# HGRN scores and scores times values: 128x128 matmuls per pair of chunks in place of 64- and 32-wide tiles

## Chip, cores and metric

One core of one Trainium2 chip runs the whole program. The metric is device time in microseconds. The kernel before takes 2924.32 us, the median of 3 runs (2922.41 to 2926.64 us). Engines are named as in the profile: PE is the matmul engine and PEld its weight loads, DVE the vector engine, ACT the scalar engine, POOL and SP the other two.

## The reference

The program is a four-part trunk over 1024 tokens of width 1024: an even layer (SSD and gMLP heads), a feed-forward layer, an odd layer (a convolution module and HGRN2 heads) and a second feed-forward layer. The change touches the HGRN2 heads of the odd layer only. There are 8 heads; in each the tokens are cut into 16 chunks of 64:

```python
qg = qv * jnp.exp(bcum - mid)
kg = k * jnp.exp(mid - bcum)
causal = jnp.tril(jnp.ones((c, c), dtype=bool))
att = jnp.where(causal, jnp.einsum("bnthk,bnshk->bnhts", qg, kg), 0.0)
o_intra = jnp.einsum("bnhts,bnshv->bnthv", att, iv)
...
def step(s, inp):
    qd, kd, vc, cd = inp
    o = jnp.einsum("blhk,bhkv->blhv", qd, s)
    s = s * cd[..., None] + jnp.einsum("blhk,blhv->bhkv", kd, vc)
    return s, o
```

So the scores of a chunk are a 64 by 64 product of `kg` and `qg` over 128 channels, kept where the key's token is not after the query's; they are multiplied with the values `iv`; the product of the queries with the running state is added. Scores between different chunks are not used.

## The kernel before

Everything is kept with channels on the 128 partitions, tokens along the free axis. Dense projections are split into a high and a low part and run as three matmuls per tile of 128 channels: `dense` (lines 149 to 151, 512 tokens at a time) and `dense_tok` (lines 160 to 162). `odd` (line 1106) runs the odd layer. For each head h it walks `hgrn_proj` (line 914), a generator over 8 units of dense work (two halves of `wf`, two halves of `wq`, four of `wig`) that yields once more at its end, and then, for h below 6, one pair of convolution channels (`conf_pair`, `conf_half`, lines 867 to 887; 4 units). Between two units `unit` (line 118) emits one step of queued small work and up to three convolution taps (`conv31`, line 889; L900, on DVE). The queued small work is `hgrn_core` (line 973) of the head before: each of its `yield`s ends a step. The tile scheduler then orders each engine's instructions by priority, mostly as they were written; weights have a higher priority.

The steps of `hgrn_core` are: transposes of `kg` (L981); the scores (L991, L993 on PE, then the masked copies L995, L998 on DVE); the state's products and its chain over the chunks in two steps (L1008 on PE, L1016 on DVE, L1017 on ACT); two empty steps; the output for two halves of 8 chunks (L1032 and L1035 on PE, L1038 on ACT, L1039 and L1040 on DVE); the norm and the store. That is 9 yields. All these matmuls have plain fp32 operands, and the trace shows two passes on PE for each.

The scores of chunk n are two matmuls: 64 keys by the chunk's last 32 queries (L991, a 128x64 tile of the array) and its first 32 keys by its first 32 queries (L993, a 128x32 tile). Even chunks land on partitions 0 to 63, odd ones on 64 to 127, so `att` of a head is 128 partitions by 8 times 64, in one buffer of [128, 512]; the two such buffers (`self.att`, lines 1110 to 1114) alternate between heads. `blk_u` is the causal mask of 64 by 64, twice (line 1256). The output step walks pairs of chunks: two matmuls of 64x64 tiles (L1032), then two of 128x64 tiles with the state (L1035), added in the same PSUM bank. PSUM has 4 banks named `mm` for dense work and 4 named `sm` for the small work.

Of the kernel before, what the change touches and what calls it, by code (L numbers as in the profile page):

```python
# [17 lines left out]
T = 1024  # L18
HALF = 512
NT = 8  # L20
# [36 lines left out]
class Trunk:  # L57
# [9 lines left out]

# [1 line left out]
    def nm(self, s):  # L69
# [27 lines left out]
    def split(self, t, h, lo):  # L97
        """t = h + lo: h holds the leading 12 bits, lo the exact remainder."""
        self.nc.scalar.copy(R(h), t)  # L99
        return self.nc.vector.tensor_tensor(R(lo), t, h, ALU.subtract)  # L100
# [17 lines left out]
    def unit(self, nsteps=1, nlow=0):  # L118
        """Called after each unit of dense work: emits queued small work."""
        for _ in range(nsteps):  # L120
            while self.steps:
                try:
                    next(self.steps[0])
                    break
                except StopIteration:
                    self.steps.popleft()
            else:
                break
        for _ in range(nlow):
            if self.lows:  # L130
                self.lows.popleft()()
# [10 lines left out]
    def dense(self, ps, w, acts, r, w0=0, ws=P, first=True, last=True):  # L142
        """ps[out channel, tokens] += W^T act over the K tiles of acts (hi, lo)."""
        wh, wl = w
        n = len(acts)
        for k, (ah, al) in enumerate(acts):
            c = slice(w0 + k * ws, w0 + k * ws + P)
            mm = self.nc.tensor.matmul
            mm(ps, R(wh[:, c]), R(ah[:, r]), start=(first and k == 0), stop=False)  # L149
            mm(ps, R(wh[:, c]), R(al[:, r]), start=False, stop=False)  # L150
            mm(ps, R(wl[:, c]), R(ah[:, r]), start=False, stop=(last and k == n - 1))  # L151

    def dense_tok(self, ps, ws, acts, t, n):
        """ps[tokens of tile t, n] = act^T W; ws are two K-half weight tiles."""
        r = slice(t * P, (t + 1) * P)
        mm = self.nc.tensor.matmul
        for k, (ah, al) in enumerate(acts):
            wh, wl = ws[k // 4]
            c = slice((k % 4) * n, (k % 4) * n + n)
            mm(ps[:, :n], R(ah[:, r]), R(wh[:, c]), start=(k == 0), stop=False)  # L160
            mm(ps[:, :n], R(ah[:, r]), R(wl[:, c]), start=False, stop=False)  # L161
            mm(ps[:, :n], R(al[:, r]), R(wh[:, c]), start=False, stop=(k == len(acts) - 1))  # L162

    def lnexp(self, after):
        """Loads the activation table set that serves both Ln and Exp, after the given instruction."""
        with self.tc.issue_after(after.ins):
            self.nc.scalar.preload_act_table_set("natural_log_exp_and_others")

    def rstd(self, src, out, scale, shape):
        """out = (src * scale + eps) ** -0.5, with one Newton step."""  # L170
        nc = self.nc
        vv = self.small(shape, "rs_v%d" % shape[1])
        tt = self.small(shape, "rs_t%d" % shape[1])
        nc.vector.tensor_scalar(vv, src, scale, EPS, ALU.mult, ALU.add)
        nc.scalar.activation(tt, vv, AF.Ln)
        nc.scalar.activation(out, tt, AF.Exp, scale=-0.5)
        nc.scalar.activation(tt, out, AF.Square)
        nc.vector.tensor_tensor(tt, tt, vv, ALU.mult)
        nc.vector.tensor_scalar(tt, tt, -0.5, 1.5, ALU.mult, ALU.add)
        nc.vector.tensor_tensor(out, out, tt, ALU.mult)  # L180

    def psum_parts(self, acc, r):
        """Sum over the partitions, given to every partition."""
        n = r.stop - r.start
# [3 lines left out]

# [1 line left out]
    def norm_start(self, X, g, split=True):  # L190
# [32 lines left out]
    def scaled_split(self, x, g, h, lo):  # L223
        """x * g = h + lo."""
        self.nc.scalar.activation(R(h), x, AF.Copy, scale=g)  # L225
        self.nc.vector.scalar_tensor_tensor(R(lo), x, g, h, ALU.mult, ALU.subtract)

    def norm_rows(self, st, square=False):
        """The norm's factor of every token, on every partition (or its square); takes the place of the sums."""
        for half in range(2):  # L230
# [6 lines left out]

# [1 line left out]
    def wino_start(self, X, g, spill):  # L239
        return dict(X=X, g=g, acc=None, spill=spill, ops={}, late=[])  # L240

    def wino_ops(self, st, r, k):
        """Operands of channel tiles k and k + 4; X is overwritten (the residual is in st["spill"])."""
        nc, X, tt = self.nc, st["X"], self.nc.vector.tensor_tensor
# [32 lines left out]

# [1 line left out]
    def out_chunk(self, wsrc, acts, X, norm=None, fill=0, segs=(hs(0), hs(1))):  # L279
        """X += W^T acts for chunks of four K tiles (wsrc, acts: one per chunk), in blocks of two output tiles.  # L280
        norm: state of the norm that follows; then segment after segment of the tokens."""
        nc = self.nc
# [33 lines left out]

# [1 line left out]
    def ffn_in(self, l, st, hid, load):  # L318
        """hid = relu(W1^T h)^2 in Winograd's form over 2 x 2 quadrants (output tiles, K halves, token halves)."""
        nc, ops, tt = self.nc, st["ops"], self.nc.vector.tensor_tensor  # L320
# [13 lines left out]
        def weights():  # L334
            """The seven operands of one unit after the other, in the order of their use."""
            def op(src):
# [120 lines left out]

# [1 line left out]
    def dt_prep(self, after):  # L459
# [53 lines left out]
    def gmlp(self, st):  # L513
# [37 lines left out]
        def first(r):  # L551
            """Operands of one segment of tokens, without the norm's factor."""
            for i in range(NT):
# [6 lines left out]
        def factors():  # L560
            """The norm's factor, tokens on the partitions."""
            ps = self.sm_ps()
# [278 lines left out]

# [1 line left out]
    def lower_bound(self):  # L843
# [70 lines left out]
    def hgrn_proj(self, h, acts):  # L914
        """Projections of head h and the elementwise work on its gates; a generator over dense units."""
        nc, a = self.nc, self.a
# [56 lines left out]
    def hgrn_core(self, h, hd):  # L973
# [9 lines left out]
        yield  # L983
        at = self.att[h % 2]
        at3 = at.rearrange("p (c t) -> p c t", t=64)
        ps = self.sm_ps()
        ps3 = ps.rearrange("p (c t) -> p c t", t=64)
        for n in range(16):
            j, p = n % 2, n // 2
            m0 = n * 64  # L990
            nc.tensor.matmul(ps[64 * j:64 * j + 64, p * 64 + 32:p * 64 + 64], kg[:, m0:m0 + 64],  # L991
                             qg[:, m0 + 32:m0 + 64], start=True, stop=True)
            nc.tensor.matmul(ps[64 * j:64 * j + 32, p * 64:p * 64 + 32], kg[:, m0:m0 + 32],  # L993
                             qg[:, m0:m0 + 32], start=True, stop=True)
        nc.vector.copy_predicated(at3[:, :, 32:64], bcast_mid(self.blk_u[:, 32:64], NT), ps3[:, :, 32:64])  # L995
        for j in range(2):
            pr = slice(64 * j, 64 * j + 32)
            nc.vector.copy_predicated(at3[pr, :, 0:32], bcast_mid(self.blk_u[pr, 0:32], NT), ps3[pr, :, 0:32])  # L998
        yield
        V = [self.slot("V"), self.slot("V")]  # L1000
# [24 lines left out]
        for half in range(2):  # L1025
            r = hs(half)
            ps = self.sm_ps()
            for c in range(4):
                p = half * 4 + c
                for j in range(2):  # L1030
                    pr = slice(64 * j, 64 * j + 64)
                    nc.tensor.matmul(ps[pr, b(c)], at[pr, p * 64:p * 64 + 64], iv[pr, b(p)], start=True, stop=False)  # L1032
                for j in range(2):
                    n = 2 * p + j
                    nc.tensor.matmul(ps[64 * j:64 * j + 64, b(c)], qg[:, n * 64:(n + 1) * 64], vv(n),  # L1035
                                     start=False, stop=True)
            s2 = self.small([P, HALF], "s2")
# [11 lines left out]
    def hgrn_load(self, h, gate):  # L1049
        """Head h's output, channels on the partitions, split."""  # L1050
        nc = self.nc
# [126 lines left out]

# [1 line left out]
    def build(self):  # L1180
# [37 lines left out]

# [1 line left out]
def layout(inputs):  # L1220
# [34 lines left out]
    blk = np.zeros((P, P), np.float32)  # L1255
    blk[:64, :64] = blk[64:, :64] = tri[:64, :64]
    r["cmat"] = np.concatenate([eye, tri, np.ones((P, P), np.float32), blk], axis=1)
# [38 lines left out]
```

## Time and profile before

| what | value |
|---|---|
| median of 3 runs | 2924.32 us |
| span of the profiled execution, first to last instruction | 2924.2 us |
| PE busy | 2892.0 us, 99% of the span |
| PEld busy | 2398.8 us, 82% |
| DVE busy | 1923.9 us, 66% |
| ACT busy | 1194.7 us, 41% |
| mean granted clock of PE | 0.985 |

The span is the only time known of the profiled execution; it lies 0.1 us from the median of the runs, so times read from the trace can be set against the runs directly. Busy times of PE are of little use by themselves, since matmuls overlap: a dense matmul lasts 0.39 us in the trace and the next starts 0.23 us after it. What a block of matmuls costs is read from the start of its first to the start of the matmul that follows it. The granted clock is 1.00 at the higher of PE's two levels (2.4 GHz) and 0.50 at the lower (1.2 GHz).

### The profile page before, as it was taken

How to read it: one execution, taken by the hardware profiler on the slowest of the kernel's cores; microseconds unless marked ns; L12 is line 12 of the kernel's file. 1: busy time of each engine (PE TensorE's matmuls, PEld its weight loads, DVE VectorE, ACT ScalarE, POOL GpSimd, SP SyncE). 2: the span in 40 equal slices, each digit the busy share in tenths (PEclk: the TensorE clock that was granted, in tenths of full speed). 3: DMA queues.
4: the chain of work that ended last, by engine and by line, in shares of the span. 5: the costliest groups of instructions: out<-in, count | busy, mean ns of one | idle time of the engine just before them, and what ended most of it. 6: DMA issues, size and time to landing. Idle time of an engine off the chain costs nothing.

```text
span 2924.2 us, 37621 instructions
## 1 busy us (share of the span) xinstructions
PE 2892.0 (99%) x15149; PEld 2398.8 (82%) x15149; DVE 1923.9 (66%) x2961; ACT 1194.7 (41%) x1964; POOL 4.0 (0%) x16
## 2 busy tenths in 40 slices
PE   8999998999999999999999999999999999999998
PEld 8988786788888888889888888888778788888887
DVE  5666878669444576537787888774587644566546
ACT  6422424237655422215343333444356655522112
POOL 0000000000000000000000000000000000000000
PEclk9999999999999999999999999998999999999999
DMA  4131425413333632212111111112512333453211
GB/s 159 45 120 62 130 87 176 134 58 108 115 116 115 209 132 100 101 51 87 61 50 50 53 57 51 50 38 66 194 51 101 116 115 116 137 202 115 87 58 59
DMA packets 100031, 287.30 MB, mean 98 GB/s; under 512 B 10768, under 2 KB 33680, under 8 KB 99856
## 3 DMA queue, kind: packets, MB, share of 16 engines
q1 hardware_dynamic: 83440, 242.47, 25.1%
q10 hardware_dynamic: 16416, 42.42, 3.7%
q8 instruction: 119, 1.95, 0.3%
q14 instruction: 56, 0.46, 0.0%
HBM read 217.61 MB, written 67.24 MB: 97 GB/s over the span
## 4 chain that ended last, share of the span: by engine, by line
PE 97%; DVE 1%; ACT 1%; DMA 0%; issue 0%; SPq 0%; DVEq 0%
PE mm L149 20%; PE mm L150 20%; PE mm L151 20%; PE mm L330 6%; PE mm L331 6%; PE mm L332 6%; PE mm L160 3%; PE mm L161 3%; PE mm L162 3%; PE sm L991 1%; PE sm L331 1%; PE sm L330 1%; PE sm L332 1%; PE sm L993 1%; PE sm L1035 1%; PE sm L1032 1%
## 5 line engine op out<-in xcount | busy, mean ns | idle before, releaser
L293 DVE TENSOR_TENSOR x<-x,mm 128x512 f32<-128x512 f32 (+1 forms) x416 | 258.7, 624 | 301.2 <-PE mm L151 292.4
L99 ACT CAST wh<-wr 128x1024 fp32r<-128x1024 f32 (+1 forms) x180 | 188.7, 1049 | 617.4 <-PE mm L150 554.0
L149 PE MATMUL mm<-fh,wh 128*128 128x512 f32 (+1 forms) x1152 | 424.9, 369 | 0.0
L151 PE MATMUL mm<-fh,wl 128*128 128x512 f32 (+1 forms) x1152 | 423.6, 368 | 0.0
L150 PE MATMUL mm<-fl,wh 128*128 128x512 f32 (+1 forms) x1152 | 422.4, 367 | 0.0
L149 PE MATMUL mm<-hh,wh 128*128 128x512 f32 x960 | 390.5, 407 | 0.0
L151 PE MATMUL mm<-hh,wl 128*128 128x512 f32 x960 | 383.4, 399 | 0.0
L150 PE MATMUL mm<-hl,wh 128*128 128x512 f32 x960 | 383.2, 399 | 0.0
L900 DVE SCALAR_TENSOR_TENSOR cy<-ag,vec,cy 128x1023 f32<-128x1023 f32 (+14 forms) x240 | 303.9, 1266 | 4.0
L100 DVE TENSOR_TENSOR wl<-wr,wh 128x1024 fp32r<-128x1024 f32 (+1 forms) x180 | 220.0, 1223 | 76.4 <-ACT wh L99 76.0
L151 PEld LDWEIGHTS mm<-fh,wl 128*128 128x128 f32 x1152 | 216.7, 188 | 38.5
L150 PEld LDWEIGHTS mm<-fl,wh 128*128 128x128 f32 x1152 | 216.5, 188 | 38.2
L149 PEld LDWEIGHTS mm<-fh,wh 128*128 128x128 f32 x1152 | 216.9, 188 | 36.9
L160 PE MATMUL mm<-wh,hh 128*128 128x256 f32 (+1 forms) x768 | 219.1, 286 | 8.6 <-ACT hh L225 8.6
L149 PEld LDWEIGHTS mm<-hh,wh 128*128 128x128 f32 x960 | 184.6, 192 | 44.7 <-issue 3.7
L150 PEld LDWEIGHTS mm<-hl,wh 128*128 128x128 f32 x960 | 184.2, 192 | 41.9 <-issue 1.8
L151 PEld LDWEIGHTS mm<-hh,wl 128*128 128x128 f32 x960 | 183.7, 191 | 42.5
L161 PE MATMUL mm<-wl,hh 128*128 128x256 f32 (+1 forms) x768 | 217.2, 283 | 0.4 <-DVE wl L100 0.4
L162 PE MATMUL mm<-wh,hl 128*128 128x256 f32 (+1 forms) x768 | 216.2, 283 | 0.0
L330 PE MATMUL mm<-T,wq 128*128 128x512 f32 x512 | 201.1, 394 | 0.6 <-ACT snap L379 0.6
L331 PE MATMUL mm<-T,wq 128*128 128x512 f32 x512 | 201.2, 394 | 0.0
L332 PE MATMUL mm<-T,wq 128*128 128x512 f32 x512 | 200.3, 393 | 0.0
(301 smaller groups left out, 5157.5 us busy)
## 6 DMA issues: line engine op xcount, KB each, us to landing
wr<-in_w_dram SPq DMA_DIRECT2D x134, 512.0 KB, 3.6
hid<-hid ACTq DMA_DIRECT2D x64, 512.0 KB, 3.5
ft<-hid SPq DMA_DIRECT2D x64, 512.0 KB, 4.7
x<-xd SPq DMA_DIRECT2D x24, 512.0 KB, 10.2
A<-acs_d SPq DMA_DIRECT2D x16, 512.0 KB, 5.9
wr<-in_wig_dram SPq DMA_DIRECT2D x16, 512.0 KB, 3.6
wr<-in_wxbc_dram SPq DMA_DIRECT2D x12, 512.0 KB, 3.5
wr<-in_wv_dram SPq DMA_DIRECT2D x8, 520.0 KB, 5.2
```

The source lines that it names most:

```text
L100: return self.nc.vector.tensor_tensor(R(lo), t, h, ALU.subtract)
L149: mm(ps, R(wh[:, c]), R(ah[:, r]), start=(first and k == 0), stop=False)
L150: mm(ps, R(wh[:, c]), R(al[:, r]), start=False, stop=False)
L151: mm(ps, R(wl[:, c]), R(ah[:, r]), start=False, stop=(last and k == n - 1))
L160: mm(ps[:, :n], R(ah[:, r]), R(wh[:, c]), start=(k == 0), stop=False)
L161: mm(ps[:, :n], R(ah[:, r]), R(wl[:, c]), start=False, stop=False)
L162: mm(ps[:, :n], R(al[:, r]), R(wh[:, c]), start=False, stop=(k == len(acts) - 1))
L293: nc.vector.tensor_tensor(X[o][:, r], X[o][:, r], ps, ALU.add)
L330: mm(ps, R(w[:, c]), R(b[:, L]), start=(first and k == 0), stop=False, skip_group_check=not first)
L331: mm(ps, R(w[:, c]), R(b[:, H]), start=False, stop=False, skip_group_check=not first)
L332: mm(ps, R(w[:, cl]), R(b[:, L]), start=False, stop=(last and k == 3), skip_group_check=not first)
L900: nc.vector.scalar_tensor_tensor(d, st[:, :T - k], w, d, ALU.mult, ALU.add)
```

## The change

The scores become one matmul per pair of chunks: 128 keys by 128 queries (both chunks), 4 of them per PSUM bank, so two banks and two steps per head. The off-diagonal 64x64 blocks are computed and not copied. `att` of a head is now two buffers of [128, 512], one for each half, each holding 4 blocks of 128x128 with zeros outside the masks; both heads in turn use the same two buffers. The mask `blk` becomes block-diagonal. The masked copies are three per half instead of three per head. Scores times values is one 128x128 matmul per pair, 4 in a row, followed by the 8 matmuls with the state in a row. `hgrn_core` has 10 yields instead of 9. Other differences in the diff are comments.

```diff
@@ hgrn_core
-        at = self.att[h % 2]
-        at3 = at.rearrange("p (c t) -> p c t", t=64)
-        ps = self.sm_ps()
-        ps3 = ps.rearrange("p (c t) -> p c t", t=64)
-        for n in range(16):
-            j, p = n % 2, n // 2
-            m0 = n * 64
-            nc.tensor.matmul(ps[64 * j:64 * j + 64, p * 64 + 32:p * 64 + 64], kg[:, m0:m0 + 64],
-                             qg[:, m0 + 32:m0 + 64], start=True, stop=True)
-            nc.tensor.matmul(ps[64 * j:64 * j + 32, p * 64:p * 64 + 32], kg[:, m0:m0 + 32],
-                             qg[:, m0:m0 + 32], start=True, stop=True)
-        nc.vector.copy_predicated(at3[:, :, 32:64], bcast_mid(self.blk_u[:, 32:64], NT), ps3[:, :, 32:64])
-        for j in range(2):
-            pr = slice(64 * j, 64 * j + 32)
-            nc.vector.copy_predicated(at3[pr, :, 0:32], bcast_mid(self.blk_u[pr, 0:32], NT), ps3[pr, :, 0:32])
-        yield
+        at = self.att
+        for half in range(2):
+            ps = self.sm_ps()
+            for c in range(4):
+                m = b(half * 4 + c)
+                nc.tensor.matmul(ps[:, b(c)], kg[:, m], qg[:, m], start=True, stop=True)
+            v4 = lambda t: t.rearrange("p (c j t) -> p c j t", j=2, t=64)
+            m4 = bcast_mid(self.blk_u, 4).rearrange("p c (j t) -> p c j t", j=2)
+            nc.vector.copy_predicated(v4(at[half])[:, :, :, 32:64], m4[:, :, :, 32:64], v4(ps)[:, :, :, 32:64])
+            for j in range(2):
+                pr = slice(64 * j, 64 * j + 32)
+                nc.vector.copy_predicated(v4(at[half])[pr, :, j, 0:32], m4[pr, :, j, 0:32], v4(ps)[pr, :, j, 0:32])
+            yield
...
-                for j in range(2):
-                    pr = slice(64 * j, 64 * j + 64)
-                    nc.tensor.matmul(ps[pr, b(c)], at[pr, p * 64:p * 64 + 64], iv[pr, b(p)], start=True, stop=False)
-                for j in range(2):
-                    n = 2 * p + j
-                    nc.tensor.matmul(ps[64 * j:64 * j + 64, b(c)], qg[:, n * 64:(n + 1) * 64], vv(n),
-                                     start=False, stop=True)
+                nc.tensor.matmul(ps[:, b(c)], at[half][:, b(c)], iv[:, b(p)], start=(c == 0), stop=False, skip_group_check=True)
+            for n in range(half * 8, half * 8 + 8):
+                pr = slice(64 * (n % 2), 64 * (n % 2) + 64)
+                nc.tensor.matmul(ps[pr, b((n // 2) % 4)], qg[:, n * 64:(n + 1) * 64], vv(n), start=False, stop=True,
+                                 skip_group_check=True)
@@ layout
-    blk[:64, :64] = blk[64:, :64] = tri[:64, :64]
+    blk[:64, :64] = blk[64:, 64:] = tri[:64, :64]
```

On PE, at the score step of head 0, the order before is the end of a dense unit and then the two small matmuls of each chunk in turn (`hh`, `hl` are the activations, `wh`, `wl` the weights; the last numbers are output partitions and columns):

```order
L149 MATMUL mm_11734<-hh_5766,wh_11682 128x512
L150 MATMUL mm_11734<-hl_5758,wh_11682 128x512
L151 MATMUL mm_11734<-hh_5766,wl_11683 128x512
L991 MATMUL sm_11762<-qg_11307,kg_11308 64x32
L993 MATMUL sm_11762<-qg_11307,kg_11308 32x32
```

The same place in the changed kernel:

```order
L151 MATMUL mm_11734<-hh_5766,wl_11683 128x512
L989 MATMUL sm_11762<-qg_11307,kg_11308 128x128 x4
L149 MATMUL mm_11797<-hh_5759,wh_11792 128x512
L150 MATMUL mm_11797<-hl_5751,wh_11792 128x512
L151 MATMUL mm_11797<-hh_5759,wl_11793 128x512
```

The 32 small matmuls have become 4, and dense work follows at once; 24 dense matmuls later the other 4 stand in the same way.

On PE, at the output step of head 0, before (the second half follows after 48 more matmuls of L160 to L162):

```order
L162 MATMUL mm_12078<-wh_11964,hl_5758 128x256
L1032 MATMUL sm_12132<-iv_11325,att_10866 64x128 x2
L1035 MATMUL sm_12132<-V_11851,qg_11307 64x128 x2
L1032 MATMUL sm_12132<-iv_11325,att_10866 64x128 x2
L1035 MATMUL sm_12132<-V_11851,qg_11307 64x128 x2
```

and in the changed kernel:

```order
L162 MATMUL mm_12112<-wh_11914,hl_5758 128x256
L1027 MATMUL sm_12166<-iv_11325,att_10866 128x128 x4
L1030 MATMUL sm_12166<-V_11860,qg_11307 64x128 x8
L1027 MATMUL sm_12186<-iv_11325,att_10868 128x128 x4
L1030 MATMUL sm_12186<-V_11861,qg_11307 64x128 x8
L149 MATMUL mm_12221<-hh_5759,wh_12210 128x512
```

The first half has moved behind the last dense unit of the projections (one more yield stands ahead of it), so the two halves now follow each other; and the kinds of matmul change once per half, not once per pair.

On DVE, from the score step of head 0 in the changed kernel (`cy` are convolution taps, `hA` and `hB` the gates of the next head):

```order
L992 COPY_PREDICATED att_10866<-cm,sm_11762 128x8x32
L995 COPY_PREDICATED att_10866<-cm,sm_11762 32x4x32 x2
L900 SCALAR_TENSOR_TENSOR cy_11619<-ag_10896,vec,cy_11619 128x1010
L900 SCALAR_TENSOR_TENSOR cy_11619<-ag_10896,vec,cy_11619 128x1009
L900 SCALAR_TENSOR_TENSOR cy_11619<-ag_10896,vec,cy_11619 128x1008
L933 TENSOR_TENSOR hA_11686<-hA_11686,hB_11687 128x1024
L992 COPY_PREDICATED att_10868<-cm,sm_11823 128x8x32
L995 COPY_PREDICATED att_10868<-cm,sm_11823 32x4x32 x2
```

Before, one set of three copies stood there, with the taps and `hA` after it; now a second set waits for the second score block.

## Rows read from the trace of the kernel before

**Rows 1.** The page, part 1 and part 4: busy time, and the chain by engine.
```profile
PE 2892.0 (99%) x15149; PEld 2398.8 (82%) x15149; DVE 1923.9 (66%) x2961; ACT 1194.7 (41%) x1964; POOL 4.0 (0%) x16
...
PE 97%; DVE 1%; ACT 1%; DMA 0%; issue 0%; SPq 0%; DVEq 0%
```
**Rows 2.** Windows, score step to score step, heads 0 to 5: busy, clock, DMA.
```profile
1481.27:1567.56 86.29, 86.29 (x551) 71.84 (x551) 76.75 (x87) 34.45 (x59) 0.20 (x1) 0.96 0.15 49
...
sum 497.34, PE 497.34 PEld 414.27 DVE 405.77 ACT 202.98 POOL 1.23; mean PE 82.89 PEld 69.05 DVE 67.63 ACT 33.83 POOL 0.20
```
**Rows 3.** Timeline of PE, score step of head 0: start, us, operation.
```profile
1480.72 0.40 PE L150 MATMUL mm<-hl,wh 128*128 128x512 f32 x1
1480.95 0.39 PE L151 MATMUL mm<-hh,wl 128*128 128x512 f32 x1
1481.27 0.30 PE L991 MATMUL sm<-qg,kg 128*64 128x32 f32 x2
...
1481.68 0.30 PE L991 MATMUL sm<-qg,kg 128*64 128x32 f32 x2
...
1488.46 0.80 PE L149 MATMUL mm<-hh,wh 128*128 128x512 f32 x1
...
1489.49 0.63 PE L151 MATMUL mm<-hh,wl 128*128 128x512 f32 x1
1489.91 0.63 PE L149 MATMUL mm<-hh,wh 128*128 128x512 f32 x1
```
**Rows 4.** Windows, the eight score steps: first, and sum.
```profile
1481.27:1488.46 7.19, 7.19 (x65) 5.72 (x64) 2.22 (x2) 5.79 (x7) 0.00 (x0) 0.86 0.23 74
...
sum 61.83, PE 61.83 PEld 49.01 DVE 14.17 ACT 42.81 POOL 0.00; mean PE 7.73 PEld 6.13 DVE 1.77 ACT 5.35 POOL 0.00
```
**Rows 5.** Windows, end of score step to end of low clock, eight heads.
```profile
1488.46:1493.25 4.79, 4.79 (x13) 3.81 (x12) 4.53 (x6) 0.00 (x0) 0.00 (x0) 0.50 0.00 0
...
sum 35.08, PE 35.08 PEld 27.95 DVE 30.35 ACT 2.61 POOL 0.00; mean PE 4.38 PEld 3.49 DVE 3.79 ACT 0.33 POOL 0.00
```
**Rows 6.** Timeline of PE, output step of head 0, first half.
```profile
1521.49 0.44 PE L1032 MATMUL sm<-iv,att 64*64 64x128 f32 x4
1521.86 0.44 PE L1035 MATMUL sm<-V,qg 128*64 128x128 f32 x4
...
1524.43 0.39 PE L160 MATMUL mm<-wh,hh 128*128 128x256 f32 x1
```
**Rows 7.** Timeline of PE, blocks of the even layer: gMLP mix, SSD diagonal.
```profile
207.51 5.52 PE L611 MATMUL sm<-wst,v 128*128 128x128 f32 x48
212.79 0.48 PE L149 MATMUL mm<-hh,wh 128*128 128x512 f32 x1
...
395.06 1.09 PE L724 MATMUL sm<-A,xd 128*64 128x128 f32 x16
396.09 0.50 PE L149 MATMUL mm<-hh,wh 128*128 128x512 f32 x1
```
**Rows 8.** Instructions of L611: ns min, median and max.
```profile
L611 PEld LDWEIGHTS sm<-wst,v x128: 186/192/193, 166.4 to 212.6; 128*128 128x128 f32 x128
L611 PE MATMUL sm<-wst,v x128: 271/275/377, 166.4 to 212.8; 128*128 128x128 f32 x128
```
**Rows 9.** Windows, transposes and outputs of head 7 without dense work; L611 block.
```profile
2057.98:2064.83 6.85, 6.85 (x73) 3.94 (x72) 2.69 (x4) 1.86 (x3) 0.00 (x0) 1.00 1.03 410
207.51:212.79 5.28, 5.28 (x50) 5.28 (x48) 4.89 (x8) 1.58 (x2) 0.00 (x0) 1.00 0.35 99
```
**Rows 10.** Instructions of L995 and L998, the masked copies: ns, counts.
```profile
L995 DVE COPY_PREDICATED att<-cm,sm x8: 440/441/444, 1488.6 to 2041.5; 128x256 f32<-128x256 uint32 x8
...
L998 DVE COPY_PREDICATED att<-cm,sm x16: 420/428/446, 1489.0 to 2042.3; 32x256 f32<-32x256 uint32 x16
```
**Rows 11.** Waits: us in total, times, longest.
```profile
DVE att L995 <- PE sm L993: 45.7, 8, 6.3
```
**Rows 12.** Windows, head 7's score step to the end of its outputs.
```profile
2034.17:2072.00 37.83, 36.14 (x248) 27.35 (x248) 20.77 (x45) 15.91 (x34) 0.00 (x0) 0.91 0.74 284
```

## The prediction

> **What bounds the kernel now.** I read the page first. PE is busy for 99% of the span and the chain that ended last runs over PE for 97% of it [rows 1]; the other engines wait for PE far more than it waits for them. So the question is what PE spends on the work that is changed, and whether another engine is close behind.
>
> For the second half of that I read the windows from one score step to the next. Heads 0 to 5, where convolution taps run beside the projections, take 497.34 us; PE fills all of it and DVE 405.77 us, 82%. Head 0 alone has 76.75 us of DVE work in 86.29 us [rows 2]. DVE has room, but not much. Part of its idle time is the wait of the masked copy for the last score matmul, 45.7 us over 8 heads, 5.7 us each [rows 11].
>
> Then the timeline of PE at the score step of head 0. Dense matmuls start 0.23 us apart; from the last of them to the first score matmul it is 0.32 us, so changing to the small tile costs 0.09 us. One chunk (L991 and L993, two passes each) takes 1481.27 to 1481.68, 0.41 us, although it streams only 32 columns per pass; 16 chunks should be done in 6.6 us. The next dense matmul starts at 1488.46, after 7.19 us, and dense matmuls are then 0.42 us apart, nearly double [rows 3]. The granted clock explains both: its mean over the step is 0.86, and after the step it is 0.50 until 1493.25 [rows 4, 5]. So the clock falls to 1.2 GHz while the array is fed with these small matmuls alone. It happens in all eight heads: the eight steps take 61.83 us [rows 4], and the stretches behind them, mostly dense work at half clock, 35.08 us [rows 5].
>
> Last, the output step. Half a head takes 1521.49 to 1524.43, 2.94 us, and its kinds of matmul change every 0.37 us [rows 6].
>
> **The change part by part.** All of it lies on PE's path in the odd layer, so what a block takes from its start to the next matmul's start counts in full.
>
> *Scores.* Removed: 61.83 us, and 8 changes to the small tile, 0.7 us. Added: 16 blocks of 4 matmuls, 8 passes each, fp32, 128x128, 128 columns. The gMLP mix has just this form: 48 passes in 212.79 - 207.51 = 5.28 us, 0.110 us a pass, at clock 1.00 [rows 7, 9]. A block is then 0.88 us and 16 are 14.1 us. Saved: 61.83 + 0.7 - 14.1 = 48.4 us.
>
> This price carries most of the forecast, so here is what speaks against it. L611's weight load lasts 0.19 us and its matmul 0.27 us [rows 8], yet they come every 0.110 us: load and multiplication of neighbours overlap. The Trainium skill's page "TensorEngine Tiling (Array Packing)" says, under Key Properties, that different tiles can execute loads and matmuls in parallel, and its Overview promises up to twofold speed for a contraction or free size of 64 or less. By that rule the small tiles are the fast form, and a full tile gives the overlap up: rival 3 below, 2936 us. By the rows a full tile overlaps as well: 2845 us. The trace does not agree with the rule here, so I take the rows.
>
> *Clock.* If the score step is two blocks of 0.88 us with 24 dense matmuls between, nothing like the thin matmuls that preceded the fall is left (in head 0 a mean of 0.86 over 7.19 us makes 2.0 us at half clock, so some 5.2 us of them came first). What shows that the new blocks keep the clock up: the 5.28 us of L611 without dense work ran at 1.00, and so did 6.85 us of transposes and outputs of head 7 [rows 9]. The 35.08 us at half clock go by at full clock: 35.08 x (1 - 0.23/0.42) = 15.9 us saved.
>
> *Output step.* Removed: 16 x 2.94 = 47.0 us. Added per half: 8 full passes, 0.88 us, one change of kind, 0.09 us, and 16 passes of 128x64 tiles in a row. SSD's diagonal has that form: 395.06 to 396.09, 1.03 us, its own change back included [rows 7]. That is 2.00 us, 32.0 us for 16. Saved: 15.0 us. Nearly as much would come from the grouping alone, since 16 small passes in a row cost 1.03 us where four times 0.37 us were paid.
>
> *Masked copies.* Three per head, 0.44 + 2 x 0.43 = 1.3 us [rows 10], become six; two of each three are half as wide. They cost between half of today's and the same, so 0.5 to 1.3 us more DVE work per head. No PE work waits for them soon: in head 0 the scores ended at 1488.46 and were read from 1521.49 on, 33 us later [rows 3, 6]. They are free as long as DVE keeps up.
>
> *The extra step.* The second score block pushes the rest of the core back by one unit. In the heads before the last, the first output half moves behind the last dense unit; the state's chain gets as many units as before, and 4 us of outputs follow each other, which rows 9 cover. For head 7, PE had 1.7 us of idle time in 37.83 us [rows 12]; now its two output halves move among the dense matmuls of the out projection. I bound this by -1.7 us (that idle time goes) and +6 us (eight links of the state chain stand bare) and take 0, because dense work now stands between chain and output.
>
> *Buffers.* `att` is no longer doubled over heads. The next head's copy must wait for this head's outputs, behind which PE has five dense units of 24 matmuls before the next score step comes: nothing. The score banks are two per head, not one, of four; each is read by DVE within a unit: nothing.
>
> Sum: 48.4 + 15.9 + 15.0 = 79.3 us. From the span of 2924.2 us, which is the runs' median to 0.1 us, that leaves **2844.9 us**.
>
> **Rivals.**
>
> *1. DVE becomes the bound.* PE would need 497.34 - 79.3 x 6/8 = 437.9 us for heads 0 to 5; DVE has 405.77 us and about 5 us of new copies, 94% of that. Head 0 would have 76.4 us of PE and 77.6 us of DVE. If the idle time that is not the wait for scores (9.5 - 5.7 = 3.8 us) also stays, such a head takes 81.4 us, 5 us more. Two heavy heads lose 10 us: 2855 us. Against it: over six heads DVE has room, PE filled every one of these windows so far [rows 2], and the wait for scores vanishes.
>
> *2. The clock still falls.* Two outputs in a row, or a score block near other small work, could be thin enough. Then the 15.9 us stay: 2861 us. Against it: rows 9.
>
> *3. A full tile does not overlap (slower).* If the new passes paid load and multiplication one after the other, 0.19 + 0.275 = 0.467 us, the 256 full passes (128 for scores, 128 for values) would cost 119.6 us instead of 28.2 us: 2936 us, 12 us slower than before. It decides from 0.42 us a pass on. For it: they read operands that ACT and DVE have just written, with four per bank. Against it: L611 at 0.110 us.
>
> *4. More gain.* If a full pass cost no more than a 128x64 one in a row (1.03/16 = 0.064 us), 256 passes would save another 11.7 us: 2833 us.
>
> **How the numbers follow.** Forecast 0.74, DVE 0.13, clock 0.08, slower 0.03, more gain 0.02. The likeliest gives 2845 us. The range reaches down to 2835 us (the tail's bound and most of rival 4) and up to 2859 us (DVE, and the tail's +6 us); the clock rival and the slow one stay out, with a little of the rest, under 2 in 10. A measurement of this kernel can tell about 0.2%, 6 us, from no change. Only rival 3 is slower: 0.03; cases 1, 2 and 4 are far below 2918 us, so faster has 0.96; 0.01 is left for same.
>
> **What would show it.** Right: each score block lasts 0.8 to 0.9 us from its start to the next dense matmul; the granted clock shows no fall between 1400 and 2100 us and its mean rises above 0.99; half a head's outputs take about 2.0 us; a head takes about 76 us. Wrong: PE waits for DVE or ACT in heads 0 to 2, dense matmuls 0.42 us apart behind the outputs, or full passes well over 0.110 us.

## The result and the profile after

The changed kernel takes **2852.68 us** (median of 4 runs, 2851.08 to 2856.86), the kernel before 2925.31 us beside it (2922.41 to 2926.64): a ratio of 0.9757, 95% interval [0.9743, 0.9771]. In a second job (the repeat, below) it took 2852.83 us (2848.45 to 2853.66), ratio 0.9749 [0.9734, 0.9763], with the same two new waits of PE, 7.7 and 1.5 us. The forecast was 2845 us, the range 2835 to 2859 us.

The profiled execution is the slowest of the first four runs, 2856.86 us with a span of 2855.1 us. So the time of a run is 1.8 us more than its span, and the span of 2924.2 us that the forecast started from belongs to a run a little above its median; as the time of a run the forecast would be some 1.8 us higher. Below, spans are set against spans.

The page of the changed kernel, part 1 and part 4, against [rows 1]:

```profile
PE 2815.4 (99%) x14637; PEld 2361.8 (83%) x14637; DVE 1927.6 (68%) x2985; ACT 1198.3 (42%) x1964; POOL 4.0 (0%) x16
...
PE 93%; DVE 5%; ACT 1%; DMA 1%; issue 1%; SPq 0%; DVEq 0%
```

PE has 76.6 us less to do and is still busy for 99% of the span. The chain that ended last now runs for 7% over DVE, ACT and a DMA, where it was 2%.

Windows of the changed kernel, first score block to first score block, heads 0 and 3 and the sum over heads 0 to 5, against [rows 2]. The columns are the length, the busy time of PE, PEld, DVE, ACT and POOL with counts, the granted clock, the DMA share and GB/s:

```profile
1482.96:1559.43 76.47, 76.47 (x488) 66.87 (x487) 75.57 (x89) 34.55 (x59) 0.20 (x1) 1.00 0.17 56
...
1712.57:1792.75 80.18, 78.67 (x488) 68.18 (x487) 67.57 (x82) 34.73 (x59) 0.20 (x1) 0.98 0.17 53
...
sum 446.09, PE 444.58 PEld 389.08 DVE 409.83 ACT 210.38 POOL 1.23; mean PE 74.10 PEld 64.85 DVE 68.30 ACT 35.06 POOL 0.21
```

Head 0 went from 86.29 to 76.47 us and runs at clock 1.00 from end to end. PE fills it, although DVE is busy for 75.57 us of it. Head 3 is 3.7 us longer than its neighbours, at a clock of 0.98; PE has 1.5 us of idle time there.

Timeline of PE in the changed kernel, the first score block of head 0, against [rows 3]:

```profile
1482.73 0.39 PE L151 MATMUL mm<-hh,wl 128*128 128x512 f32 x1
1482.96 1.05 PE L989 MATMUL sm<-qg,kg 128*128 128x128 f32 x8
1483.77 0.48 PE L149 MATMUL mm<-hh,wh 128*128 128x512 f32 x1
```

The block takes 1482.96 to 1483.77, 0.81 us, for 8 passes: 0.10 us each. It starts 0.23 us after the dense matmul before it, the usual distance: there is no gap for a change of tile. Fifteen of the 16 blocks take 0.80 or 0.81 us, one 0.98 us.

Timeline of PE in the changed kernel, the output step of head 0, both halves, against [rows 6]:

```profile
1521.06 1.05 PE L1027 MATMUL sm<-iv,att 128*128 128x128 f32 x8
1522.04 1.09 PE L1030 MATMUL sm<-V,qg 128*64 128x128 f32 x16
1523.06 1.16 PE L1027 MATMUL sm<-iv,att 128*128 128x128 f32 x8
1524.15 1.09 PE L1030 MATMUL sm<-V,qg 128*64 128x128 f32 x16
1525.17 0.50 PE L149 MATMUL mm<-hh,wh 128*128 128x512 f32 x1
```

A head's outputs take 4.11 us in place of 5.88. The eight falls of the clock behind the score steps [rows 5] are gone.

Two things are there that were not there before. PE's waits in the changed kernel (total, times, longest):

```profile
PE sm L1055 <- DMA ol<-hgd: 7.6, 1, 7.6
...
PE sm L1030 <- ACT V L1014: 1.5, 2, 1.0
```

The first stands at the end of the heads. Timeline of PE there (in brackets the idle time before an operation, and what ended it):

```profile
1962.53 1.09 PE L1030 MATMUL sm<-V,qg 128*64 128x128 f32 x16
1971.25 1.94 PE L1055 MATMUL sm<-cm,ol 128*128 128x128 f32 x8 [7.63 <-DMA ol<-hgd]
1972.98 1.91 PE L1027 MATMUL sm<-iv,att 128*128 128x128 f32 x8
1974.83 1.83 PE L1030 MATMUL sm<-V,qg 128*64 128x128 f32 x16
1976.59 0.50 PE L149 MATMUL mm<-hyh,wh 128*128 128x512 f32 x1
```

L1055 transposes a head's output that was stored to DRAM and is loaded again for the out projection (`hgrn_load`, L1050). PE's order has these transposes between the two output halves of head 6, so the second half waits with them, and all dense work behind it. Where the load was is on SP's queue. Its timeline in the changed kernel (start, time to the end of the last of the group):

```profile
1925.94 38.35 SPq L107 DMA_DIRECT2D wr<-in_woh_dram  x4
1964.38 1.33 SPq L1050 DMA_DIRECT2D ol<-hgd  x3
```

Four loads of the out projection's weights stand ahead of the first `ol`. The later ones wait until a buffer `wr` is free; the first load of `ol` is issued at 1964.38, and PE goes on 6.9 us later.

The second is in head 3. Timeline of DVE in the changed kernel, the end of the state's chain there:

```profile
1751.98 1.25 DVE L900 SCALAR_TENSOR_TENSOR cy<-ag,vec,cy 128x1001 f32<-128x1001 f32 x1
1753.15 1.22 DVE L100 TENSOR_TENSOR wl<-wr,wh 128x1024 fp32r<-128x1024 f32 x1
1754.29 0.34 DVE L1013 SCALAR_TENSOR_TENSOR Z<-Z,hcf,sm 128x128 f32<-128x128 f32 x1
1754.55 1.22 DVE L100 TENSOR_TENSOR wl<-wr,wh 128x1024 fp32r<-128x1024 f32 x1
1755.68 0.34 DVE L1013 SCALAR_TENSOR_TENSOR Z<-Z,hcf,sm 128x128 f32<-128x128 f32 x1
```

and of PE at the same time:

```profile
1753.69 0.88 PE L1030 MATMUL sm<-V,qg 128*64 128x128 f32 x12
1755.12 0.43 PE L1030 MATMUL sm<-V,qg 128*64 128x128 f32 x2 [0.55 <-ACT V L1014]
1756.51 0.43 PE L1030 MATMUL sm<-V,qg 128*64 128x128 f32 x2 [0.96 <-ACT V L1014]
1756.87 0.50 PE L149 MATMUL mm<-hh,wh 128*128 128x512 f32 x1
```

The last links of the chain (L1013) come one at a time between convolution taps and weight splits, DVE without a gap. PE needs the last two states before they are there: its last state products take 1753.69 to 1756.87, 3.2 us in place of 1.0.

Behind both waits the clock is low. Windows of the changed kernel, dense work behind head 3's outputs, and from the load's arrival to the next dense matmul:

```profile
1756.87:1761.30 4.43, 4.43 (x14) 3.47 (x13) 4.43 (x7) 2.29 (x4) 0.20 (x1) 0.62 0.43 162
1971.25:1976.59 5.34, 5.34 (x33) 4.93 (x33) 1.50 (x2) 1.37 (x2) 0.00 (x0) 0.52 0.14 55
```

The work of the second window takes 2.95 us at full clock in the run e11_pool_load below (1964.07 to 1967.02), so the low clock costs 2.4 us more.

### The profile page after: what moved, and what is told of

The parts are those of the page before. It is cut to its first block, busy times and chain, and to the rows that moved or that the text cites. A ratio compares the mean times of both kernels' runs of the same rounds, so it can differ in the third digit from the quotient of the medians.

```text
span 2855.1 us, 36628 instructions
## 1 busy us (share of the span) xinstructions
PE 2815.4 (99%) x14637; PEld 2361.8 (83%) x14637; DVE 1927.6 (68%) x2985; ACT 1198.3 (42%) x1964; POOL 4.0 (0%) x16
## 4 chain that ended last, share of the span: by engine, by line
PE 93%; DVE 5%; ACT 1%; DMA 1%; issue 1%; SPq 0%; DVEq 0%
PE mm L149 19%; PE mm L151 19%; PE mm L150 19%; PE mm L330 6%; PE mm L331 6%; PE mm L332 6%; PE mm L160 3%; PE mm L161 3%; PE mm L162 3%; DVE cy L900 2%; PE sm L331 1%; PE sm L330 1%; PE sm L332 1%; PE sm L724 1%; PE sm L186 1%
## 5 line engine op out<-in xcount | busy, mean ns | idle before, releaser
L149 PE MATMUL mm<-hh,wh 128*128 128x512 f32 x960 | 384.5, 400 | 0.0
L100 DVE TENSOR_TENSOR wl<-wr,wh 128x1024 fp32r<-128x1024 f32 (+1 forms) x180 | 219.9, 1223 | 75.4 <-ACT wh L99 75.1
L160 PE MATMUL mm<-wh,hh 128*128 128x256 f32 (+1 forms) x768 | 219.7, 287 | 9.6 <-ACT hh L225 8.7
L162 PE MATMUL mm<-wh,hl 128*128 128x256 f32 (+1 forms) x768 | 216.7, 283 | 0.0
```

## Experiments

The theory after the result: PE's stream sets the time, and the terms for scores, clock and outputs are right; what is missing is lost in two new waits that the tenth step brings (the runs bear this out for the first wait only). The rivals: DVE has become the bound of the heavy heads; the new passes cost more than their blocks show; the gain of the outputs is one of the full tile, not of the grouping. The kernel before took 2923.79 us in the first job (7 runs) and 2924.95 us in the second.

**e1_nine_steps**: the changed kernel with one empty step less, so nine as before.

```diff
@@ hgrn_core
-        yield
         yield
         o = self.slot("o")
```

> The changed kernel with one of the two empty steps of hgrn_core left out, so that the core has nine steps again, as before the change. Theory (the tenth step pushed head 7's schedule: on SP two more weight loads stand ahead of the first load of a stored head, so PE waits 7.6 us for it and runs 10 us at half clock): the wait of the transposes for the load of hgd and the fall of the clock near 1966 us are gone, some 10 us, 2843 us. Rival (the load is late whatever the order, or the outputs, one unit earlier, now wait for the state's chain): 2853 us or more.

Measured: **2843.44 us** (2841.47 to 2846.86), ratio 0.9726 [0.9711, 0.974]. It beats both kernels: 9.2 us less than the changed one. Its SP queue:

```profile
1920.13 14.37 SPq L107 DMA_DIRECT2D wr<-in_woh_dram  x2
1934.60 0.38 SPq L1049 DMA_DIRECT2D ol<-hgd  x1
```

Two weight loads, not four, stand ahead of the first `ol`; it is issued 30 us earlier, and PE no longer waits for it: its transposes start at 1959.89. The second `ol` is issued at 1960.67, behind two more weight loads, and PE waits 1.7 us for that one. Timeline of PE, and the window from there on:

```profile
1967.37 1.06 PE L1054 MATMUL sm<-cm,ol 128*128 128x128 f32 x8 [1.69 <-DMA ol<-hgd]
```

```profile
1967.37:1973.55 6.18, 6.18 (x45) 5.34 (x45) 4.47 (x12) 3.40 (x8) 0.00 (x0) 1.00 0.96 351
```

No low clock follows this wait. Head 3's wait is gone as well, and the clock does not fall between 1400 and 2100 us. Heads 0 to 4 take 76.4 to 76.7 us. So leaving the tenth step out is worth 9.2 us here. This run takes both waits away together; the next two take one each.

**e11_pool_load**: ten steps, only the load of `ol` goes through another queue (and the small memset that stood on that queue moves to DVE).

```diff
-        nc.gpsimd.memset(vv(0), 0.0)
+        nc.vector.memset(vv(0), 0.0)
...
-            nc.sync.dma_start(o, self.hgd[h])
+            nc.gpsimd.dma_start(o, self.hgd[h])
```

> The changed kernel with its ten steps; only the queue of the last stage's loads is another: ol is loaded by GpSimd's queue instead of SP's, and the memset of V's first block is done by VectorE instead of GpSimd, so that nothing stands ahead of the loads on GpSimd. Theory (the first ol load is late because two woh loads stand ahead of it on SP and wait for a wr buffer): the load starts soon after its head was stored, at about 1923 us instead of 1964 us, PE's 7.6 us wait for it is gone, and so is the fall of the clock at 1966 us (2.5 us); 2852.7 - 10 = about 2843 us. Rival (the wait is only moved: PE comes to the second half of head 6's outputs before VectorE or ScalarE are done, whatever the load does): another wait of several us stands at the same place and the time stays at 2850 us or above.

Measured: 2844.94 us (2844.33 to 2847.36), ratio 0.9726 [0.9712, 0.9741]. Timeline of POOL and then of PE:

```profile
1926.67 0.66 POOL L1050 DMA_DIRECT2D ol<-hgd  x1 [944.17 <-ACT kt L982]
```

```profile
1963.05 1.09 PE L1030 MATMUL sm<-V,qg 128*64 128x128 f32 x16
1964.07 1.09 PE L1055 MATMUL sm<-cm,ol 128*128 128x128 f32 x8
...
1967.02 0.50 PE L149 MATMUL mm<-hyh,wh 128*128 128x512 f32 x1
```

The load is issued at 1926.67, PE does not wait, and the clock does not fall there. Expected were 10 us, measured 7.8 us; heads 4 and 5 are 1.5 us longer together (77.18 and 60.62 us, against 76.46 and 59.84), and PE waits for V there too, 0.3 us each. Head 3 keeps its wait (80.47 us, 0.3 us more). That SP's order is the cause of the long wait is shown; the rival's other wait at that place did not appear.

**e8_half_taps**: ten steps, and less work for DVE beside the heads: 15 of the 31 taps are left out.

```diff
-        for k in range(31):
+        for k in range(16):
```

> The changed kernel with its ten steps, and 16 of the 31 taps of the convolution that VectorE works through beside the heads; the other 15 taps of every channel are left out. Theory (head 3's wait for the multiply of V is VectorE being late, as taps stand between the links of the chain; in heads 0 to 2 TensorE still sets the length): PE's waits for ScalarE at V in the heads are gone with the half clock behind them, no head of the first five is longer than 76.7 us, none shorter than 76.2 us, and the 7 us wait for the load of ol stays, if the order on SP is the same; about 2849 us. Rival (VectorE sets the length of heads 0 to 2 as well): heads 0 to 2 shrink clearly below 76 us.

Measured: 2845.96 us in one run. Windows of heads 0 and 3:

```profile
1477.68:1554.15 76.47, 76.47 (x487) 66.87 (x486) 48.10 (x64) 34.38 (x59) 0.20 (x1) 1.00 0.17 56
...
1707.29:1783.74 76.45, 76.45 (x487) 66.90 (x486) 48.12 (x64) 34.36 (x59) 0.21 (x1) 1.00 0.18 56
```

With DVE at 48 us a head, head 0 takes 76.47 us as before, to the hundredth, and head 3 has come down from 80.18 to 76.45 us. So a DVE that is busy for 75.6 of 76.5 us costs nothing in head 0, and one that is busy for 67.6 us costs 3.7 us in head 3: what stands between the chain's links decides, not the busy share. The load's wait stays, 6.6 us. The single time is 3 us below what was expected. Some 2.3 us of that is not of the taps' doing: the first score block starts at 1477.68, against 1479.95 in the repeat, and from 455 to 500 us, in the even layer, the mean clock is 0.96 against 0.89. The rest lies behind the heads, where the wait is 1 us shorter and the low clock at it lasts 6.8 us in place of 10.2.

**e10_scores_twice**: nine steps, each score matmul issued twice.

```diff
-                nc.tensor.matmul(ps[:, b(c)], kg[:, m], qg[:, m], start=True, stop=True)
+                for _ in range(2):
+                    nc.tensor.matmul(ps[:, b(c)], kg[:, m], qg[:, m], start=True, stop=True)
```

> The changed kernel with nine steps, in which every score matmul is issued twice into the same place (same output). It doubles the 0.81 us of a score block, 16 blocks. Theory (TensorE's stream alone sets the time in the heads, so an added matmul pass is paid in full): 16 x 0.81 = 13 us more than the 2843.4 us of the nine-step kernel, 2856.5 us, and a head is 1.6 us longer (78.1 us instead of 76.5). Rival (VectorE, busy 75.5 of 76.5 us in the first heads, sets a head's length there): the added passes are taken up in heads 0 to 2, some 5 us of them, and the time is 2851 us or less.

Measured: 2856.0 us (2854.06 to 2856.58), ratio 0.976 [0.9744, 0.9777]; 12.6 us more than e1_nine_steps. Timeline of PE and the window of head 0:

```profile
1480.08 1.95 PE L990 MATMUL sm<-qg,kg 128*128 128x128 f32 x16
1481.78 0.48 PE L149 MATMUL mm<-hh,wh 128*128 128x512 f32 x1
```

```profile
1480.08:1558.33 78.25, 78.25 (x503) 68.66 (x502) 77.52 (x90) 34.80 (x59) 0.21 (x1) 1.00 0.17 55
```

The doubled block takes 1.70 us, 0.89 us more, and head 0 is 1.78 us longer, two such blocks. An added pass is paid in full in the heavy heads too. DVE is not their bound.

**e3_scores_only**: the new scores with the old output step, pair by pair on small tiles.

```diff
-                nc.tensor.matmul(ps[:, b(c)], at[half][:, b(c)], iv[:, b(p)], start=(c == 0), stop=False, skip_group_check=True)
-            for n in range(half * 8, half * 8 + 8):
...
+                for j in range(2):
+                    pr = slice(64 * j, 64 * j + 64)
+                    nc.tensor.matmul(ps[pr, b(c)], at[half][pr, c * P + 64 * j:c * P + 64 * j + 64], iv[pr, b(p)], start=True, stop=False)
+                for j in range(2):
+                    n = 2 * p + j
+                    nc.tensor.matmul(ps[64 * j:64 * j + 64, b(c)], qg[:, n * 64:(n + 1) * 64], vv(n),
+                                     start=False, stop=True)
```

> The changed kernel with the old output step (64x64 and 128x64 tiles in turn, pair by pair) on the new scores. Theory (the output step is worth 15 us by itself, 2.94 against 2.0 us per half, and the scores with the clock the rest): 2853 + 15 = 2868 us. Rival (5.9 us of alternating small matmuls in a row now let the clock fall in each head, 3 to 10 us of half clock): 2880 us or more. Rival (PE waits for something else behind the output step, so its price is hidden): 2853 us.

Measured: 2865.95 us (2862.06 to 2866.45), ratio 0.9797 [0.9781, 0.9814]. Windows of head 0's outputs and of the whole of head 3:

```profile
1519.15:1525.03 5.88, 5.88 (x66) 3.14 (x65) 5.25 (x9) 3.42 (x8) 0.18 (x1) 1.00 0.54 178
1716.14:1794.43 78.29, 78.29 (x504) 66.45 (x502) 66.37 (x81) 34.57 (x59) 0.20 (x1) 1.00 0.17 54
```

The scores alone bring 57.8 us, the outputs the other 13.3 us (2865.95 - 2852.68); by the blocks the outputs are 8 x (5.88 - 4.11) = 14.2 us. That the two agree is in part chance: here head 3 does not wait, though this kernel has ten steps (78.29 us, and head 0 78.34), while the load's wait is here as well (6.3 us, with 13.7 us of low clock). Head 0 against head 0, the outputs are worth 78.34 - 76.47 = 1.87 us, 15.0 us for eight heads. The outputs on small tiles, 5.88 us in a row, leave the clock at 1.00, as the new ones do.

**e4_grouped_small**: the changed kernel with the values' product on 64x64 tiles, but eight matmuls in a row.

```diff
-                nc.tensor.matmul(ps[:, b(c)], at[half][:, b(c)], iv[:, b(p)], start=(c == 0), stop=False, skip_group_check=True)
+                for j in range(2):
+                    pr = slice(64 * j, 64 * j + 64)
+                    nc.tensor.matmul(ps[pr, b(c)], at[half][pr, c * P + 64 * j:c * P + 64 * j + 64], iv[pr, b(p)],
+                                     start=(c == 0), stop=False, skip_group_check=True)
```

> The changed kernel with scores times values as eight 64x64 matmuls in a row per half in place of four 128x128. Theory (the gain of the output step comes from grouping, not from the full tile): a block of 16 passes in a row costs as SSD's diagonal, about 1.0 us, against 0.93: 2854 us. Rival (the full tile is what helps): 0.18 us per pass as before the change, 1.5 us a block, 2862 us or more. Rival (small tiles packed in a row are faster than a full tile): 0.55 us a block, 2847 us.

Measured: 2851.93 us (2848.76 to 2854.93), ratio 0.9753 [0.9739, 0.9768], the same as the changed kernel. Timeline of PE, first half of head 0's outputs:

```profile
1521.07 0.28 PE L162 MATMUL mm<-wh,hl 128*128 128x256 f32 x1
1521.28 1.09 PE L1029 MATMUL sm<-iv,att 64*64 64x128 f32 x16
1522.30 1.09 PE L1033 MATMUL sm<-V,qg 128*64 128x128 f32 x16
```

Sixteen small passes take 1.02 us, the eight full ones of the changed kernel 0.98 or 1.09 us; the small ones also need 0.09 us more after the dense matmul (1521.07 to 1521.28, where the usual distance is 0.12). So the outputs gain by the grouping, and the full tile adds little: head 3 takes 77.25 us here, 2.9 us less than in the changed kernel, and without that the small form would be some 2 us slower (an estimate: 2.9 less the 0.75 us between the medians). The Trainium skill, page "TensorEngine Tiling (Array Packing)", section Overview, promises up to twofold speed for a dimension of 64 or less; this run agrees for one pass (0.064 us against 0.12), but the 64-wide tiles need twice the passes here. It holds for passes of one kind in a row: pair by pair, four such passes cost 0.37 us [rows 6], 0.09 us each.

**e5_thin_split**: the kernel before, its thin scores cut into two steps of eight chunks, one empty step less.

```diff
@@ hgrn_core (before)
+            if n == 7:
+                yield
...
-        yield
```

> The kernel before, its thin score matmuls unchanged, but in two steps of eight chunks with a dense unit between (one empty step left out, so nine steps). It tells the clock's share from that of the form. Theory (the fall of the clock comes from 5 us of thin matmuls in a row): each half takes 3.3 us at full clock and no fall follows: 8 x (7.73 - 6.75) + 16 = 24 us less, 2901 us. Rival (the clock falls all the same, behind one of the halves): 2925 us, or slower with two falls per head.

Measured: 2909.87 us (2905.13 to 2913.21), ratio 0.9951 [0.9936, 0.9965]. Windows of head 0's first half, its second half, and what follows:

```profile
1481.05:1484.33 3.28, 3.28 (x34) 2.62 (x33) 3.28 (x3) 3.26 (x5) 0.00 (x0) 1.00 0.09 11
1490.08:1493.36 3.28, 3.28 (x33) 2.62 (x32) 0.00 (x0) 1.44 (x2) 0.00 (x0) 1.00 0.00 0
1493.36:1496.86 3.50, 3.50 (x11) 2.76 (x10) 3.28 (x6) 0.00 (x0) 0.00 (x0) 0.52 0.02 5
```

Between the two expectations in time; the rival's mechanism came, at a smaller price. Each half runs at full clock, but behind the second the clock falls all the same, for 3.4 us, in heads 0 to 5; head 6 has no fall, and in head 7 the scheduler put the halves together again (7.91 us, and a fall of 6.8 us). Shorter thin blocks made the falls shorter, not rare. The run measures what the prediction worked out as 6.6 us: a head's thin scores cost 6.56 us at full clock. So of the scores' gain, 8 x (6.56 - 1.62) = 39.5 us is the form; the clock gave 61.83 - 8 x 6.56 = 9.4 us within the steps and some 16 us behind them.

## Why the prediction was right, and where 8 us went

*Scores* (48.4 us): right in mechanism and size. A block costs 0.81 us where 0.88 was taken from L611; e10_scores_twice shows that it is paid in full. The gap of 0.09 us that was removed has not come back.

*Clock* (15.9 us): right. In the runs with the new scores no fall follows a score block or an output step, unless PE had waited there. The forecast that the clock shows no fall at all between 1400 and 2100 us was wrong: there are two, each with a wait of PE; the mean rose to 0.993 all the same.

*Output step* (15.0 us): right, 14.2 us by the blocks and 15.0 us by head 0 of e3_scores_only. The prediction's remark that the grouping alone would bring nearly as much is shown by e4_grouped_small.

*The extra step*: **this term failed.** It was bounded from -1.7 to +6 us by the state's chain of head 7 and taken as 0. The kernel without the step is 9.2 us shorter (e1_nine_steps), and the loss comes by another way than the one that was priced: 7.8 us come back when the load of `ol` alone is moved (e11_pool_load). The step was followed past PE's and DVE's work, but not past SP's queue: one unit later means two weight loads more ahead of the first `ol`. And the wait was then put as if only the waiting work were late; PE's order has half of head 6's outputs and all dense work behind those transposes, and the clock falls while it waits.

*The state's chain*: the prediction says that it "gets as many units as before". That holds up to the first output half only; the second half has lost the dense unit ahead of it. In head 3, the chain's last products (first line), its last link and the start of the second output half, in the kernel before and then in the changed one:

```profile
1763.08 1.16 PE L1008 MATMUL sm<-iv,kt 64*128 64x128 f32 x14
1781.52 0.34 DVE L1016 SCALAR_TENSOR_TENSOR Z<-Z,hcf,sm 128x128 f32<-128x128 f32 x1
1790.05 0.44 PE L1032 MATMUL sm<-iv,att 64*64 64x128 f32 x4
```

```profile
1732.49 1.16 PE L1005 MATMUL sm<-iv,kt 64*128 64x128 f32 x14
1752.61 1.16 PE L1027 MATMUL sm<-iv,att 128*128 128x128 f32 x8
1755.68 0.34 DVE L1013 SCALAR_TENSOR_TENSOR Z<-Z,hcf,sm 128x128 f32<-128x128 f32 x1
```

The room shrank from 27.0 to 20.1 us. The chain took 18.8 us before and takes 23.5 us now, which the old room would have held. The nine-step kernel has no more room (20.2 us), but its chain ends in 19.4 us there, and PE does not wait; e3_scores_only and e4_grouped_small, with ten steps, lose nothing and 0.7 us in head 3. So head 3's 3.7 us come from the lost unit together with the order on DVE, not from the tenth step by itself.

*Rival 1, DVE*: in heads 0 to 2, where it was placed, it did not come, with DVE busy for 94 to 99%. In head 3, with DVE at 67.6 us, the same mechanism costs 3.7 us for a reason that no sum of busy times shows: which instructions stand ahead of the last links of a chain that has no room left.

*Rival 3, the slower side*: a full pass took 0.10 us in the scores and 0.12 to 0.14 us in the outputs, far from the 0.42 us from which it would have decided. *Rivals 2 and 4* did not come either: the heads run at 1.00 but for head 3, and a full pass costs more than a small one in a row, 0.10 to 0.14 against 0.064 us.

From the first score block to the end, the sum reads so:

| from the first score block on | us |
|---|---|
| before, 2924.2 - 1481.27 | 1442.9 |
| forecast, less 79.3 | 1363.6 |
| head 3, 80.18 - 76.47 | +3.7 |
| wait for `ol` | +7.6 |
| half clock behind it, 5.34 - 2.95 | +2.4 |
| rest | -5.2 |
| after, 2855.1 - 1482.96 | 1372.1 |

The rest is a gain from head 5 on: heads 0 to 4 together save 49.6 us when head 3's 3.7 us are added back (432.11 - 386.25 + 3.71), which is 5/8 of the forecast. Of the rest, 2.4 us are two waits of PE in the kernel before, from head 6's score step on, that the changed kernel does not have (1.5 us for `hyh`, L225, and 0.9 us for `cl`, L100); the other 2.8 us were not traced further. Nobody forecast this gain, so it is luck that the total came within 8 us and not 13. The start of the program took 1.7 us more in this execution (1482.96 against 1481.27), with a short fall of the clock at 20.5 us; the repeat did not have it (1479.95), so it is no part of the change.

## What to carry to other kernels

Small matmuls that let the clock fall are priced wrongly by their columns: replace them by full tiles that compute some waste, and put those that stay small in rows of one kind. When a change adds a step to a software pipeline, walk every queue that the later work is moved past, the DMA queue first, and count the room of every chain up to its last reader: a load behind two others that wait for buffers can cost more than the step's own work, and a queue with nothing ahead of it cures it. A busy share of 99% on a second engine may cost nothing, and one of 84% may cost microseconds: look at what stands ahead of the link that is waited for.

## What the runs showed of the hardware

- Two waits of PE in head 3, 1.5 us together, were followed by dense work at a mean clock of 0.62 for 4.43 us, so that the head lost 3.7 us, 2.2 us of it at the waits and 1.5 us at the low clock: a wait can cost PE more than its own length. The repeat shows the same head at 80.15 us. It need not: no fall followed the single wait of 1.7 us in e1_nine_steps, nor the one in e10_scores_twice.
- The thin scores let the clock fall with PE shown as busy throughout, also in two blocks of 3.28 us (e5_thin_split, behind the second); score blocks of full tiles of 0.81 us, and of 1.70 us (e10_scores_twice), did not in these runs, and neither did 5.88 us of 64-wide outputs (e3_scores_only).
- A full tile follows dense matmuls at the usual distance; a 64-wide tile starts 0.09 us late.
